# Two small edits to a hybrid GLA and MLP block: more tiny buffers ahead of the second MLP product's operands, and one engine for each PSUM bank of transposed tokens

## The chip, the cores and the metric

The kernel runs on one core of a Trainium2 chip. A core has TensorE (PE in the profile, with its weight loads apart as PEld), VectorE (DVE), ScalarE (ACT), GpSimd (POOL) and SyncE (SP, which here issues nearly all DMAs). The metric is the device time of one execution in microseconds. Three timed runs of the kernel before gave 2401.96, 2402.1 and 2409.05 us; the median is 2402.1 us.

## The reference, cut to what matters

One layer (DEPTH 1) over 2048 latent tokens and 256 context tokens of width 1024: a normed and modulated input goes through bidirectional gated linear attention (GLA), then through a squared-ReLU MLP of width 4096, each added to the residual; a last RMSNorm gives the output.

```python
a_lat = modulate(rmsnorm(h_lat, norm1_g[i]), mod_l[0], mod_l[1])
a_ctx = modulate(rmsnorm(h_ctx, norm1_g[i]), mod_c[0], mod_c[1])
o_ctx, o_lat = gla_mixer(a_ctx, a_lat, gla_w_in[j], ..., gla_w_o[j], need_ctx)
h_lat = h_lat + mod_l[2] * o_lat
h_lat = h_lat + mod_l[5] * sqrelu_mlp(modulate(rmsnorm(h_lat, norm2_g[i]), mod_l[3], mod_l[4]),
                                      mlp_w1[i], mlp_w2[i])
return rmsnorm(h_lat, final_g)

def sqrelu_mlp(h, w1, w2):
    return jnp.square(jax.nn.relu(h @ w1)) @ w2
```

## The kernel before, in words

Every large product is done in fp32r with both operands split into a high and a low part, and three matmuls for each pair (`mm3`, lines 83 to 87: high by high, high by low, low by high). In these calls the first operand named is the stationary one (it is loaded into the array, PEld) and the second is the moving one, which streams through. The profile prints them the other way round: `yp<-w,hs` is a product into `yp` with `w` moving and `hs` stationary.

The program has four stages, one after another.

1. Attention's first stage, from 0 to some 866 us: projections and the backward scan, chunk by chunk, with the partial results stored in DRAM (`sp_d`, `q_d`). Its matmuls have 256 columns.
2. Attention's second stage, from some 866 to 1130 us, over 16 chunks of 128 tokens. `front(ch)` loads `uu`, `o`, `rr` and `qf` of a chunk, advances the forward states `xf0` to `xf3` with `uu` (line 705) and makes `o`. `turn_o` transposes `o` on PE through two PSUM tiles `pt` (line 724) and splits it into `onh` (ACT, line 725) and `onl` (DVE, line 726). `back(ch)` multiplies `onh` and `onl` (stationary) by `wo` (moving, 512 columns), adds the residual, and norms to `hn`. `turn(ch - 1, hn)` transposes `hn` of the chunk before through two PSUM tiles `pt` as well (line 777), and empties them into `a2` with the scale and shift of the second norm: eight instructions of 128x128, four on ACT (line 782) and four on DVE (line 785). `give` then splits the result for the MLP.
3. The MLP's first product, 1130 to 1758 us: seven Strassen products, with slices of `w1` stationary and the tokens (`h2` and `ht`) moving, 512 columns, then the squared ReLU (`sq`).
4. The MLP's second product, 1760 to 2391 us: seven Strassen products again. `load_hs` brings `hs` (stationary) and `load_w2` brings `w` (moving, 512 columns); 2688 matmuls in all. The adds, the last norm and the output follow for each block of tokens.

The order on each engine is set by the tile framework's scheduler, which goes by the order of the code and by the offsets of `tc.high_priority`. A buffer of a pool that is used again waits for its readers. The pool `pw` of the second stage has two PSUM banks, and both `turn` and `turn_o` take their `pt` from it: each uses two, so PE can put the transposes of `o` into a bank only when ACT and DVE have emptied it of `hn`. The framework also keeps two engines from working on one PSUM bank at a time: the first ACT instruction on a bank of `turn` waits for the DVE instruction ahead of it, and the next DVE instruction for ACT. `uu` has one buffer, so the DMA for the next chunk's `uu` starts when the last of the four instructions of line 705 has read it.

A pool's buffers lie one behind another in SBUF, in the order in which the pools are opened. In the last stage `n_w` (the moving `w`) comes first, then `n_x`, then `n_wk` with the small tiles (`junk`, `ssq`, `rsv`, `rsr`, `tmp`), then `n_wr`, `n_hr`, `n_acc` and `n_h` (the stationary `hs`). So the count of `ssq` buffers, each of which takes 32 bytes in a partition, sets the byte at which all that follows begins. `ssq` holds sums of squares (line 1106 and line 1115).

Of the kernel before, what the change touches and what calls it, by code (L numbers as in the profile page):

```python
# [8 lines left out]
F32 = mybir.dt.float32  # L9
# [8 lines left out]
P = 128  # L18
# [19 lines left out]
def kernel(  # L38
# [110 lines left out]
    def held(shape, dtype, name, n):  # L149
        return [hold.tile([P] + shape, dtype, tag="hb", name=name) for _ in range(n)]  # L150
# [10 lines left out]
    with ExitStack() as sa:  # L161
# [3 lines left out]
        wk = sa.enter_context(tc.tile_pool(name="a_wk", bufs=2))  # L165
# [492 lines left out]
    with ExitStack() as sb:  # L658
        wkx = sb.enter_context(tc.tile_pool(name="b_wkx", bufs=2, reuse_waits="tile"))
        wk2 = sb.enter_context(tc.tile_pool(name="b_wk2", bufs=2, reuse_waits="tile"))  # L660
        wk = sb.enter_context(tc.tile_pool(name="b_wk", bufs=2, reuse_waits="tile"))
# [97 lines left out]
        def give(b, cp, i, src):  # L759
            if b == 0 and i in (IB11, IB21, IT1):  # L760
                if cp == 0:
                    h2_block(i)
                for j in range(2):
                    dh, dl = (t_[j][:, cp] for t_ in h2[i])
                    nc.scalar.copy(dh, src[:, 2 * j:2 * j + 2])
                    nc.gpsimd.tensor_sub(dl, src[:, 2 * j:2 * j + 2], dh.bitcast(F32))
            else:
                nc.sync.dma_start(t_d[b, i, cp], src)

        def turn(ch, hn):  # L770
            b, cp = ch // (2 * NCP), ch // 2 % NCP
            a_, = held([2, 4, P], F32, "a2", 1)
            for k4 in range(2):
                pt = pw.tile([P, 4, P], F32, tag="t", name="pt")
                for kk in range(4):
                    k = 4 * k4 + kk
                    nc.tensor.transpose(pt[:, kk, :], hn[:, k * P:(k + 1) * P], ident)
                a2 = a_[:, k4]
                for kk in range(4):
                    k = 4 * k4 + kk  # L780
                    if kk % 2:
                        nc.scalar.activation(a2[:, kk], pt[:, kk], AF.Identity, scale=s2[:, k:k + 1],
                                             bias=b2[:, k:k + 1])
                    else:
                        nc.vector.tensor_scalar(a2[:, kk], pt[:, kk], s2[:, k:k + 1], b2[:, k:k + 1],
                                                op0=ALU.mult, op1=ALU.add)
                if ch % 2 == 0:
                    give(b, cp, (IB11, IB21)[k4], a2)
            if ch % 2 == 0:
                even[0] = a_  # L790
                return
            e_ = even[0]
            t1 = wkx.tile([P, 4, P], F32, tag="t1", name="t1", bufs=1)
            nc.vector.tensor_sub(t1, a_[:, 0], e_[:, 0])
            give(b, cp, IT1, t1)
            nc.vector.tensor_sub(e_[:, 0], a_[:, 1], t1)
            give(b, cp, IT2, e_[:, 0])
            give(b, cp, IB22, a_[:, 1])
            nc.vector.tensor_sub(a_[:, 0], a_[:, 1], a_[:, 0])
            give(b, cp, IT3, a_[:, 0])  # L800
            nc.vector.tensor_sub(e_[:, 1], e_[:, 1], e_[:, 0])
            give(b, cp, IT4, e_[:, 1])
# [10 lines left out]
        for ch in range(1, NCH):  # L813
            if ch == NCH - 1:
                first_w.append(load_w1(0))
            nxt = front(ch + 1) if ch + 1 < NCH else None
            hn, on = back(ch, *on, hn, o_next=nxt)
        turn(NCH - 1, hn)

    scst.close()  # L820
# [189 lines left out]
    with ExitStack() as sm:  # L1010
        wp = sm.enter_context(tc.tile_pool(name="n_w", bufs=16, reuse_waits="tile"))
        xp = sm.enter_context(tc.tile_pool(name="n_x", bufs=2, reuse_waits="tile"))
        wk = sm.enter_context(tc.tile_pool(name="n_wk", bufs=2, reuse_waits="tile"))
# [9 lines left out]
        def load_w2(i, f):  # L1023
            raw = wr.tile([P, 512], F32, tag="wr", name="w2r")
            if i in (1, 2, 3):
                f_, n = ((f, 0), (f + NFP, 0), (f + NFP, 1))[i - 1]
                nc.sync.dma_start(raw, mlp_w2[f_ * P:(f_ + 1) * P, n * 512:(n + 1) * 512])
            else:
                nc.sync.dma_start(raw, wt_d[{5: 0, 6: 1, 7: 2, 4: 3}[i], f])
            w_ = wp.tile([P, 2, 512], F32R, tag="w", name="w2")  # L1030
            nc.scalar.copy(w_[:, 0], raw)  # L1031
            (nc.vector if f % 4 else nc.gpsimd).tensor_sub(w_[:, 1], raw, w_[:, 0].bitcast(F32))  # L1032
            return w_[:, 0], w_[:, 1]

        def load_hs(b, i, q, fq):
            raw = hr.tile([P, FQ, 256], F32, tag="hr", name="hsr")
            n = {1: 0, 2: 1, 4: 2, 5: 3, 6: 4, 7: 5, 3: 6}[i]
            nc.sync.dma_start(raw, hs_d[b, n, q, :, fq * FQ:(fq + 1) * FQ, :])
            h_ = hp.tile([P, 2, FQ, 256], F32R, tag="h", name="hs")
            nc.scalar.copy(h_[:, 0], raw)  # L1040
            nc.vector.tensor_sub(h_[:, 1], raw, h_[:, 0].bitcast(F32))  # L1041
            return h_[:, 0], h_[:, 1]
# [22 lines left out]
        for b in range(NB):  # L1065

            acc = [[None] * 4 for _ in range(2)]
            ssqs = [None] * 4
            for i in (1, 2, 6, 5, 3, 7, 4):
                w2 = []  # L1070
                for q in range(2):
                    yps = [py.tile([P, 512], F32, tag="y", name="yp") for _ in range(2)]
                    for fq in range(NFP // FQ):
                        with tc.high_priority(offset=150):
                            if q == 0:
                                w2 += [load_w2(i, fq * FQ + f) for f in range(FQ)]
                            hi, lo = load_hs(b, i, q, fq)
                        for f in range(FQ):
                            wh, wl = w2[fq * FQ + f]
                            for s in range(2):  # L1080
                                sl = slice(s * P, (s + 1) * P)
                                mm3(yps[s], hi[:, f, sl], lo[:, f, sl], wh, wl, fq == 0 and f == 0,
                                    fq == NFP // FQ - 1 and f == FQ - 1)
                    if b == 0 and i == 1 and q == 0:
                        nc.sync.dma_start(g2t.rearrange("p n e -> p (n e)"), g_d[1])
                        nc.sync.dma_start(fgt.rearrange("p n e -> p (n e)"), final_g.partition_broadcast(P))
                    for s in range(2):
                        t = 2 * q + s
                        ps = yps[s]
                        row0 = b * MB + 2 * t * P  # L1090
                        row1 = row0 + P
                        if i == 1:
                            acc[1][t] = acp.tile([P, 2, 512], F32, tag="acc", name="acc")
                            nc.scalar.copy(acc[1][t][:, 0], ps)
                        elif i == 2:
                            acc[0][t] = acp.tile([P, 2, 512], F32, tag="acc", name="acc")
                            nc.vector.tensor_add(acc[0][t][:, 0], ps, acc[1][t][:, 0])
                        elif i == 6:
                            nc.vector.tensor_add(acc[1][t][:, 0], ps, acc[1][t][:, 0])
                        elif i == 5:  # L1100
                            nc.vector.tensor_add(acc[1][t][:, 1], ps, acc[1][t][:, 0])
                        elif i == 3:
                            a = acc[0][t]
                            nc.vector.tensor_add(a[:, 1], ps, acc[1][t][:, 1])
                            residual(row0, a)
                            ssq = wk.tile([P, 3], F32, tag="ssq", name="ssq", bufs=6)
                            sumsq(a, ssq, 0)
                            sumsq(a, ssq, 1)
                            finish(row0, a, ssq)
                        elif i == 7:  # L1110
                            a = acc[1][t]
                            nc.vector.tensor_add(a[:, 0], ps, a[:, 0])
                            nc.vector.tensor_add(a[:, 1], ps, a[:, 1])
                            residual(row1, a)
                            ssqs[t] = wk.tile([P, 3], F32, tag="ssq", name="ssq", bufs=6)
                            sumsq(a, ssqs[t], 1)
                        else:
                            a = acc[1][t]
                            tmp = wk.tile([P, 512], F32, tag="tmp", name="tmp")
                            nc.vector.tensor_mul(tmp, ps, g2t[:, 0])  # L1120
                            nc.vector.tensor_add(a[:, 0], tmp, a[:, 0])
                            sumsq(a, ssqs[t], 0)
                            finish(row1, a, ssqs[t], b == NB - 1 and t == 3)
# [29 lines left out]
```

## Time and profile before

The profiled execution took 2402.64 us, of which 2400.9 us are the span from its first to its last instruction. The mean granted clock of TensorE in it is 0.987 of full speed.

| engine | busy us | share of the span | instructions |
|---|---|---|---|
| PE | 2305.0 | 96% | 13250 |
| PEld | 2002.9 | 83% | 13250 |
| DVE | 1618.3 | 67% | 2410 |
| ACT | 1233.4 | 51% | 2223 |
| POOL | 525.5 | 22% | 658 |

The DMA engines moved 456.82 MB in the span, 190 GB/s in the mean. Matmuls overlap in this profile: a 512-column matmul is shown with 0.39 us while the next starts some 0.23 us after it, so the pace of PE is read from the starts of matmuls or from how many fall into a stretch, not from their durations.

### The profile page before, as it was taken

To read this page: it belongs to the slowest core of one execution; us is meant where nothing else is said; L and a number is where in the kernel's file an instruction comes from. 1 tells how busy PE (TensorE), PEld (TensorE's weight loads), DVE (VectorE), ACT (ScalarE), POOL (GpSimd) and SP (SyncE) were. 2 spreads that over 40 slices of the span, in tenths; PEclk is the share of its full clock that TensorE was granted. 3 is DMA by queue.
4 is the path that set the end of the run, shared out by engine and by line. 5 is a ranking of instruction groups with operands and counts; after the bars stand their busy time and mean duration, and the time that the engine had idled before them with its cause. 6 is when DMAs were issued, how large, how long until landed. Compare 5 with 4: busy or idle time off the path is not lost.

```text
span 2400.9 us, 36220 instructions
## 1 busy us (share of the span) xinstructions
PE 2305.0 (96%) x13250; PEld 2002.9 (83%) x13250; DVE 1618.3 (67%) x2410; ACT 1233.4 (51%) x2223; POOL 525.5 (22%) x658
## 2 busy tenths in 40 slices
PE   6999999999999988999899999999999999999998
PEld 4899999999999977777688887888878888888886
DVE  7855777787765577777866768766565458554484
ACT  6544455555555545554655556555454344443351
POOL 2333344334433423321000000000011121211131
PEclk8999999999999989999999999999999999999999
DMA  8222454454433266775966678676596458655471
GB/s 275 87 89 95 140 175 155 149 172 141 159 121 117 84 218 209 237 259 195 294 202 206 215 225 264 213 228 202 171 327 216 167 188 298 216 194 203 164 272 71
DMA packets 364635, 456.82 MB, mean 190 GB/s; under 512 B 23164, under 2 KB 268996, under 8 KB 364456
## 3 DMA queue, kind: packets, MB, share of 16 engines
q1 hardware_dynamic: 361784, 446.14, 56.1%
q0 software_dynamic: 2416, 8.07, 1.1%
q8 instruction: 104, 1.70, 0.3%
q14 instruction: 75, 0.61, 0.1%
q10 hardware_dynamic: 256, 0.29, 0.0%
HBM read 318.10 MB, written 136.31 MB: 189 GB/s over the span
## 4 chain that ended last, share of the span: by engine, by line
PE 48%; issue 4%; DVE 4%; DMA 4%; POOL 1%; ACT 1%; SPq 0%; POOLq 0%; DVEq 0%; ACTq 0%
PE yp L86 9%; PE yp L85 9%; PE yp L84 9%; PE pa L84 4%; PE pa L86 4%; PE pa L85 4%; PE pb L84 2%; PE pb L86 2%; PE pb L85 2%; DMA uu<-sp_d 2%; PE pc L84 1%; PE pc L86 1%; PE pc L85 1%; DMA w2r<-in_mlp_w_dram 1%; POOL rsr L95 1%
## 5 line engine op out<-in xcount | busy, mean ns | idle before, releaser
L84 PE MATMUL yp<-w,hs 128*128 128x512 f32 x896 | 353.6, 395 | 2.6 <-ACT hs L1040 2.6
L86 PE MATMUL yp<-w,hs 128*128 128x512 f32 x896 | 353.8, 395 | 1.3 <-DVE hs L1041 1.3
L85 PE MATMUL yp<-w,hs 128*128 128x512 f32 x896 | 353.7, 395 | 0.0
L1032 POOL TENSOR_TENSOR w<-w2r,w 128x512 fp32r<-128x512 f32 x56 | 98.3, 1756 | 1050.3 <-ACT w L1031 1035.7
L345 POOL TENSOR_TENSOR wl<-wraw,wh 128x1024 fp32r<-128x1024 f32 x95 | 236.1, 2505 | 207.5 <-ACT wh L343 205.9
L1041 DVE TENSOR_TENSOR hs<-hsr,hs 128x1024 fp32r<-128x1024 f32 x112 | 139.8, 1251 | 146.4 <-ACT hs L1040 146.3
L1040 ACT CAST hs<-hsr 128x1024 fp32r<-128x1024 f32 x112 | 117.0, 1046 | 200.7 <-PE yp L86 140.4
L84 PEld LDWEIGHTS yp<-w,hs 128*128 128x128 f32 x896 | 168.0, 187 | 44.6 <-ACT hs L1040 3.0
L86 PEld LDWEIGHTS yp<-w,hs 128*128 128x128 f32 x896 | 167.9, 187 | 43.2 <-DVE hs L1041 1.7
L85 PEld LDWEIGHTS yp<-w,hs 128*128 128x128 f32 x896 | 167.9, 187 | 41.6
L1031 ACT CAST w<-w2r 128x512 fp32r<-128x512 f32 x224 | 137.1, 618 | 113.4 <-PE yp L86 100.3
L1032 DVE TENSOR_TENSOR w<-w2r,w 128x512 fp32r<-128x512 f32 x168 | 135.9, 823 | 62.3 <-ACT w L1031 59.3
L84 PE MATMUL vps<-wh,ah 128*128 128x256 f32 x576 | 164.5, 286 | 0.4 <-DVE qr L509 0.4
L85 PE MATMUL vps<-wl,ah 128*128 128x256 f32 x576 | 164.1, 285 | 0.0
L86 PE MATMUL vps<-wh,al 128*128 128x256 f32 x576 | 162.9, 283 | 0.0
L84 PE MATMUL kqps<-ah,wh 128*128 128x256 f32 x544 | 155.8, 286 | 0.0
L85 PE MATMUL kqps<-al,wh 128*128 128x256 f32 x544 | 154.8, 285 | 0.0
L86 PE MATMUL kqps<-ah,wl 128*128 128x256 f32 x544 | 154.1, 283 | 0.3 <-DVE wl L345 0.3
L84 PE MATMUL pa<-ht,w 128*128 128x512 f32 x384 | 149.7, 390 | 3.3 <-DVE z L981 1.7
L85 PE MATMUL pa<-ht,w 128*128 128x512 f32 x384 | 149.4, 389 | 0.0
L86 PE MATMUL pa<-ht,w 128*128 128x512 f32 x384 | 149.4, 389 | 0.0
L84 PE MATMUL rps<-wh,ah 128*128 128x256 f32 x512 | 146.3, 286 | 0.0
(1278 smaller groups left out, 6384.3 us busy)
## 6 DMA issues: line engine op xcount, KB each, us to landing
hsr<-hs_d SPq DMA_DIRECT2D x112, 512.0 KB, 4.5
w2r<-in_mlp_w_dram SPq DMA_DIRECT2D x160, 256.0 KB, 5.2
wraw<-in_gla_w_in_dram SPq DMA_DIRECT2D x64, 512.0 KB, 3.6
w1r<-in_mlp_w_dram SPq DMA_DIRECT2D x64, 512.0 KB, 4.6
hs_d<-z SPq DMA_DIRECT2D x128, 256.0 KB, 3.8
w2r<-wt_d SPq DMA_DIRECT2D x128, 256.0 KB, 3.8
hs_d<-hs SPq DMA_DIRECT2D x96, 256.0 KB, 3.1
sp_d<-sp SPq DMA_DIRECT2D x60, 384.0 KB, 2.4
```

The lines of the kernel that those rows point to most:

```text
L84: nc.tensor.matmul(ps, sh, mh, start=start, stop=False, skip_group_check=skip)
L85: nc.tensor.matmul(ps, sh, ml, start=False, stop=False, skip_group_check=skip)
L86: nc.tensor.matmul(ps, sl, mh, start=False, stop=stop, skip_group_check=skip)
L95: nc.gpsimd.tensor_tensor(r[:, :w], v[:, :w], mhalf[:, :w], op=ALU.pow)
L345: eng.tensor_sub(wl[:, half * 4:half * 4 + 4, :], raw, hs.bitcast(F32))
L1031: nc.scalar.copy(w_[:, 0], raw)
L1032: (nc.vector if f % 4 else nc.gpsimd).tensor_sub(w_[:, 1], raw, w_[:, 0].bitcast(F32))
L1040: nc.scalar.copy(h_[:, 0], raw)
L1041: nc.vector.tensor_sub(h_[:, 1], raw, h_[:, 0].bitcast(F32))
```

## The change

`ssq` gets 12 buffers in place of 6. Six more buffers of 32 bytes move everything behind them in the last stage by 192 bytes. In the built programs the six `hs` buffers begin at byte 170464 + 8192 n of each partition before, and at 170656 + 8192 n after; the moving `w` stays at 16544 + 4096 n. Of these addresses the rest by 512 is what the prediction speaks of: `hs` goes from 480 to 160, `w` is at 160, and the slices that single matmuls take are whole multiples of 512 bytes further on. In the third stage both the stationary `w1` and the moving `h2` and `ht` are at 160. In the second stage the stationary `onh` and `onl` and the moving `wo` are both at 480. In the first stage `vps` has both operands at 160, and `pu_` has its moving `v` at 160 and its stationary `kt` at 224. None of these is moved by the change.

In `turn`, the first PSUM tile (k4 = 0) is now emptied by DVE alone and the second (k4 = 1) by ACT alone; before, each was emptied by both in turns.

```diff
@@ turn
-                    if kk % 2:
+                    if k4:
                         nc.scalar.activation(a2[:, kk], pt[:, kk], AF.Identity, scale=s2[:, k:k + 1],
                                              bias=b2[:, k:k + 1])
                     else:
...
@@ last stage, i == 3
-                            ssq = wk.tile([P, 3], F32, tag="ssq", name="ssq", bufs=6)
+                            ssq = wk.tile([P, 3], F32, tag="ssq", name="ssq", bufs=12)
...
@@ last stage, i == 7
-                            ssqs[t] = wk.tile([P, 3], F32, tag="ssq", name="ssq", bufs=6)
+                            ssqs[t] = wk.tile([P, 3], F32, tag="ssq", name="ssq", bufs=12)
```

The counts of instructions are the same on every engine, and POOL and SP have the same order as before. ACT, for the second stage's even chunks (here the one whose tokens are in `a_12013`; the names in brackets are the engines whose progress the instruction waits for):

```order
-L782 ACTIVATE a_12013<-pt,b_96,s_95 128x128 [waits DVE_49] x2
-L765 CAST h_11345<-a_12013 128x256 [waits Activation_49]
+L782 ACTIVATE a_12013<-pt,b_96,s_95 128x128 [waits PE_49]
+L782 ACTIVATE a_12013<-pt,b_96,s_95 128x128 x3
+L765 CAST h_11345<-a_12013 128x256 [waits DVE_49]
 L765 CAST h_11362<-a_12013 128x256 [waits Activation_49]
-L782 ACTIVATE a_12013<-pt,b_96,s_95 128x128 [waits DVE_49] x2
-L765 CAST h_11346<-a_12013 128x256 [waits Activation_49]
+L765 CAST h_11346<-a_12013 128x256 [waits DVE_49]
 L765 CAST h_11363<-a_12013 128x256 [waits Activation_49]
 L725 CAST onh<-pt 128x512 [waits PE_49] x2
```

The four ACT instructions on `pt` stand together now and wait for PE's transposes alone; two of the casts behind them wait for DVE. DVE, for the same chunk (`xf_102` and `xf_103` are the states `xf0` and `xf1`):

```order
 L713 SCALAR_TENSOR_TENSOR o<-o,rsr,rr 128x256 x4
 L745 TENSOR_TENSOR xt<-yp,xt 128x512
-L785 TENSOR_SCALAR a_12013<-pt,s_95,b_96 128x128 x2
+L785 TENSOR_SCALAR a_12013<-pt,s_95,b_96 128x128 x4
 L705 SCALAR_TENSOR_TENSOR xf_102<-xf_102,ff,uu 128x256
-L785 TENSOR_SCALAR a_12013<-pt,s_95,b_96 128x128 x2
 L705 SCALAR_TENSOR_TENSOR xf_103<-xf_103,ff,uu 128x256
 L726 TENSOR_TENSOR onl<-pt,onh 128x512 x2
```

All four DVE instructions on `pt` now stand ahead of the first instruction that needs `uu`; before, two stood behind it. PE, at the second chunk of the second stage, the one place where its order in that stage differs:

```order
 L85 MATMUL yp<-wo_11059,onh 128x512
 L86 MATMUL yp<-wo_11058,onl 128x512
-L724 MATMUL pt<-ident,o 128x128 x4
+L724 MATMUL pt<-ident,o 128x128 x8
 L84 MATMUL yp<-wo_11060,onh 128x512
-L724 MATMUL pt<-ident,o 128x128 x4
 L85 MATMUL yp<-wo_11061,onh 128x512
 L86 MATMUL yp<-wo_11060,onl 128x512
```

The eight transposes of `o` follow each other there as in the other chunks; before, a matmul stood between the two banks.

## Rows read from the trace of the kernel before

**Rows 1.** Windows: us, busy us of each engine, PEclk, DMA share, GB/s.

```profile
900.00:1120.00 220.00, 204.47 (x1052) 166.56 (x1051) 169.52 (x345) 117.95 (x311) 58.56 (x90) 0.99 0.69 231
913.20:916.20 3.00, 3.00 (x10) 2.52 (x11) 1.38 (x2) 1.25 (x3) 0.73 (x1) 0.50 0.13 25
1160.00:1760.00 600.00, 592.57 (x2610) 489.03 (x2608) 416.86 (x637) 351.24 (x587) 3.93 (x3) 1.00 0.69 222
1500.00:1600.00 100.00, 100.00 (x443) 82.79 (x442) 68.77 (x108) 57.21 (x97) 0.00 (x0) 1.00 0.67 214
1770.00:2390.00 620.00, 620.00 (x2659) 496.87 (x2658) 353.10 (x374) 255.23 (x383) 114.25 (x94) 1.00 0.60 209
```

**Rows 2.** Groups by line, PE: count, busy us, mean ns, idle before.

```profile
L84 PE MATMUL yp<-w,hs 128*128 128x512 f32 x896 | 353.6, 395 | 2.6 <-ACT hs L1040 2.6
```

**Rows 3.** Timeline of PE, fourth stage: start us, duration us, instruction.

```profile
1899.75 0.39 PE L84 MATMUL yp<-w,hs 128*128 128x512 f32 x1
...
1902.32 0.39 PE L86 MATMUL yp<-w,hs 128*128 128x512 f32 x1
```

**Rows 4.** Timeline of PE, third stage.

```profile
1702.20 0.39 PE L84 MATMUL pb<-h,w 128*128 128x512 f32 x1
...
1704.92 0.39 PE L84 MATMUL pa<-ht,w 128*128 128x512 f32 x1
```

**Rows 5.** Timeline of PE, second stage.

```profile
1112.08 0.39 PE L84 MATMUL yp<-wo,onh 128*128 128x512 f32 x1
...
1114.80 0.39 PE L84 MATMUL yp<-wo,onh 128*128 128x512 f32 x1
```

**Rows 6.** Timeline of PE, first stage, `vps`.

```profile
420.00 0.28 PE L86 MATMUL vps<-wh,al 128*128 128x256 f32 x1
...
421.79 0.28 PE L86 MATMUL vps<-wh,al 128*128 128x256 f32 x1
```

**Rows 7.** Timeline of PE, first stage, `pu_`.

```profile
425.98 0.28 PE L86 MATMUL pu__5242<-v__5105,kt 128*128 128x256 f32 x1
...
426.32 0.28 PE L86 MATMUL pu__5242<-v__5105,kt 128*128 128x256 f32 x1
```

**Rows 8.** Waits, 900 to 1120 us: total us, times, longest us.

```profile
ACT a L782 <- DVE a L785: 64.5, 26, 4.1
...
DVE xf L705 <- DMA uu<-sp_d: 7.0, 9, 2.3
...
PE pt L724 <- ACT a L782: 6.7, 8, 2.9
```

**Rows 9.** Timeline of PE, 905 to 917 us.

```profile
909.34 0.66 PE L724 MATMUL pt<-ident,o 128*128 128x128 f32 x4 [0.47 <-ACT a L782]
...
913.14 1.12 PE L724 MATMUL pt<-ident,o 128*128 128x128 f32 x4 [2.91 <-ACT a L782]
```

**Rows 10.** Timeline of DVE, 905 to 917 us.

```profile
908.39 0.72 DVE L785 TENSOR_SCALAR a<-pt,s,b 128x128 f32<-128x128 f32 x2
911.39 0.88 DVE L705 SCALAR_TENSOR_TENSOR xf<-xf,ff,uu 128x256 f32<-128x256 f32 x2 [2.28 <-DMA uu<-sp_d]
...
914.91 0.69 DVE L726 TENSOR_TENSOR onl<-pt,onh 128x512 fp32r<-128x512 f32 x1 [0.63 <-ACT onh L725]
```

**Rows 11.** Timeline of all engines, 942 to 962 us.

```profile
942.48 0.72 DVE L785 TENSOR_SCALAR a<-pt,s,b 128x128 f32<-128x128 f32 x2
...
944.71 0.48 DVE L705 SCALAR_TENSOR_TENSOR xf<-xf,ff,uu 128x256 f32<-128x256 f32 x1 [1.52 <-DMA uu<-sp_d]
...
945.55 0.81 ACT L782 ACTIVATE a<-pt,b,s 128x128 f32<-128x128 f32 x2 [1.23 <-DVE a L785]
...
946.07 1.09 PE L724 MATMUL pt<-ident,o 128*128 128x128 f32 x8 [1.14 <-ACT a L782]
...
959.55 0.48 DVE L705 SCALAR_TENSOR_TENSOR xf<-xf,ff,uu 128x256 f32<-128x256 f32 x1 [0.24 <-DMA uu<-sp_d]
```

**Rows 12.** Chain that ended last, 930 to 1010 us: start us, us, piece.

```profile
937.27 7.35 DMA uu<-sp_d
```

## The prediction

> **What bounds the kernel now.** I read the windows of each stage first, to see where PE has idle time, then the timeline of PE in each stage for its pace, then the waits of the second stage and the chain there. In the fourth stage PE never idles: 620.00 us busy of 620 [rows 1]. So the time of that stage is the count of matmuls times their pace, and no engine or DMA sets it; DVE is busy for 353 and ACT for 255 of those 620 us, and the DMA engines for 0.60 [rows 1]. The third stage is nearly the same, 592.57 of 600. The second stage is another kind: PE is busy for 204.47 of 220 us there [rows 1], and the reader should see that what it waits for at `pt` is an ACT instruction of line 782, 6.7 us in eight waits, while ACT for its part waited 64.5 us for DVE's line 785 [rows 8].
>
> **The pace of PE in the two MLP stages.** A window counts the matmuls that run at either edge too, each 0.39 us long [rows 2 to 4], so the pace is the window plus 0.39 us over the count. Fourth stage: 620.39 / 2659 = 233.3 ns. Third stage, in a window without idle time: 100.39 / 443 = 226.6 ns [rows 1]. The starts say the same: 11 steps from 1899.75 to 1902.32 are 2.57 us, 233.6 ns each [rows 3]; 12 steps from 1702.20 to 1704.92 are 2.72 us, 226.7 ns each [rows 4]. The clock is 1.00 in both stretches, the shape is the same (128x128 stationary, 512 columns of fp32r), and neither waits. What differs is where the operands lie: rests of 480 (stationary) and 160 (moving) by 512 bytes in the fourth stage, 160 and 160 in the third.
>
> The second stage tells which of these counts. There both operands have the rest 480, and 12 steps from 1112.08 to 1114.80 are again 2.72 us, 226.7 ns [rows 5]. So a stationary operand at 480 is not slow by itself, nor a moving one at 160 (the third stage has it), nor a moving operand that lies in one piece (the second stage) against one in four pieces (the third). Only the pairing of the fourth stage, 480 against 160, is seen at 233.3. The change makes this pair 160 and 160, the third stage's.
>
> **The change part by part.**
>
> First, `ssq` with 12 buffers. It adds no instruction, DMA or wait; POOL and SP keep their order. It moves `hs`, `w2r`, `hsr` and the accumulators by 192 bytes. Cost of the move: PE's pace goes from 233.3 to 226.6 ns, 6.7 ns for each of the 2659 matmuls of the window, 17.8 us. The 29 others lie in the first microseconds of the stage, where PE waits for the first operands or runs slowly, and I count nothing for them. Bounds: nothing (0), if what I take for the pairing is something else of the fourth stage; 17.8 us if it is the pairing; on the other side see the second rival. I take 17.8, the end to which all three 512-column rows point. What is late next: `hs` and `w` must come 3% faster. The third stage ran with PE full at a DMA share of 0.69 and 222 GB/s, and the fourth needs 209 x 233.3 / 226.6 = 215 GB/s [rows 1], so nothing is late.
>
> Second, the banks in `turn`. Counts and durations stay: four instructions on each engine. Before, ACT's first stands behind DVE's first on the same bank and DVE stands behind its other work, so both banks become free late. After, ACT's four wait for PE alone and are done early; DVE's four take 0.40 + 3 x 0.32 = 1.36 us at a stretch (two take 0.72, the second adds 0.32) [rows 10, 11].
>
> An even chunk, at 942 us: DVE begins at 942.48 and would be done at 943.84. Before, two of its four stood behind an instruction that waited 1.52 us for `uu` (944.71), so ACT's last began after 945.55 and PE, ready at 946.07 - 1.14 = 944.93, waited 1.14 us [rows 11]. That wait goes whole, and with it what follows it: `onh`, `onl`, the residual, `hn`, and the last reader of `uu`. This matters because `uu` has one buffer and its DMA (7.35 us at this place) lies on the chain [rows 12]: what comes sooner here also starts the next `uu` sooner, so the gain isn't given back at once.
>
> An odd chunk, at 958 us: DVE goes on with the differences of tokens, and its own idle time before `uu` is only 0.24 us [rows 11]. Its sum of work is unchanged, and PE then waits for `onl` in place of `pt`. There I win 0.24 us, not PE's wait.
>
> The first place, 905 to 917 us: PE waited 0.47 and 2.91 us [rows 9], and after the second its clock was 0.50, the lower level of 1.2 GHz, for the ten instructions of 913.2 to 916.2 [rows 1]. Four of them are transposes, 0.66 us at the earlier place [rows 9], six are matmuls of 0.227 us; together 2.0 us where 3.00 passed, so the clock cost 1.0. After the change PE waits for DVE's third and fourth at most, 908.39 + 1.04 = 909.4, and doesn't stop between the banks. But `onl` still stands behind the two instructions that wait for `uu` until 911.39: they end at 912.27, and the two of `onl` (0.69 and some 0.6) at 913.5, where the second ended at 915.60 before [rows 10]. I win 2.1 us, not 4.4.
>
> The sum of the second edit: of the 6.7 us of waits, 3.4 are at the first place (2.1 won) and 3.3 at six others. Of the 3.3 I take two thirds, 2.2, as a choice between the even kind (all) and the odd kind (little). Together 4.3 us. Bounds: at the best all 6.7 and the 1.0 of the clock, 7.7. Below nothing: the first reader of `uu` now stands behind two more of line 785, 0.64 us later, in chunks where `uu` has landed already; DVE waited for `uu` 9 times [rows 8], so in some 6 of the 15 chunks it could cost 0.64 each, 3.8 us slower, if every delay went into the chain. I take 4.3, nearer to the rows of waits than to this end, because DVE's sum of work stays. At the last chunk, where weights for the third stage are prepared between the same instructions, one is moved by one place, at most 0.4 us either way; I take 0.
>
> The sum against the profiled execution's own time: 2402.6 - 17.8 - 4.3 = 2380.5 us. That execution stands 0.5 us above the median of 2402.1, so on the median's scale 2380.0 us. The 1.7 us around the span, and the ten microseconds after the last matmul, stay.
>
> **The rivals.**
>
> The address does nothing for PE. For it: nothing in the profile names an address, and the fourth stage differs from the third in other things too (what DVE, ACT and POOL do beside PE). Against it: in the second stage DVE and ACT do yet other things, and the pace is the third stage's. Then only the second edit is left: 2402.1 - 4.3 = 2397.8 us, no change by the bound below. The Trainium skill speaks for this rival: "SBUF — State Buffer", section "Who interferes with whom", gives PE one read port for the moving operand and an independent one for weight loads, and says that PE never waits on anyone; "TensorE: Matmul & The Clock Gate", section "Back-to-back issue gap", makes the gap a matter of the columns alone. By these the two MLP stages would have one pace, and the edit would be worth nothing; the trace has two paces at one shape and one clock, so I give the rule a small chance.
>
> Equal rests are the slow kind. This one ends on the other side. In the first stage, at 256 columns, `vps` with both operands at 160 takes 15 steps in 1.79 us, 119.3 ns [rows 6], and `pu_` with 160 and 224 takes 3 steps in 0.34 us, 113.3 ns [rows 7]. So there the unequal pair is faster by 6.0 ns. If that held in the fourth stage, 2688 x 6.0 = 16.1 us would be lost: 2402.1 + 16.1 - 4.3 = 2413.9 us. It would decide as soon as it cost over 1.6 ns a matmul (4.3 / 2688). Against it: at 512 columns every row goes the other way, and the runs of `pu_` are six matmuls long.
>
> The `uu` loop takes back what `pt` gives. If each of the 14 loads of `uu` became later by the 0.64 us of two more line-785 instructions, the second stage would be 9.0 us longer in place of 4.3 shorter: 2402.1 - 17.8 + 9.0 = 2393.3 us. For it: the chain goes through these DMAs [rows 12]. Against it: where `uu` is waited for, the four are done before it lands (943.84 against 944.71).
>
> The first edit doing other than it says is not a case of its own: the addresses are those of the built program.
>
> **How the numbers follow.** A measurement of this kernel tells about 0.3%, 7.2 us, from no change. Chances: the forecast 0.86; the address does nothing 0.07; the `uu` loop 0.04, which is still faster by 0.4%; equal rests slow 0.03. So faster 0.90, same 0.07, slower 0.03. The likeliest case alone reaches from 2402.1 - 17.8 - 7.7 = 2376.6 to 2402.1 - 17.8 + 3.8 = 2388.1. The range of 8 in 10 takes that in and a little of each side, for a pace that lies between the two levels or a start of the third stage that moves: 2375 to 2391 us.
>
> **What would show it right or wrong.** In the changed kernel's windows, 600 us inside the fourth stage should count 600.39 / 0.2266 = 2649 matmuls instead of 600.39 / 0.2333 = 2573, and starts should stand 226.7 ns apart. If they stand 233.3 apart, the first step is wrong; at 239, the second rival is right. In the second stage the waits of PE at `pt` should nearly vanish and ACT's wait for DVE's line 785 with them, the clock should not fall at 913 us, and PE should wait for `onl` in places instead; if the stage from 900 us to the last `yp<-wo` is longer than before, the `uu` loop has won. The prediction fails as a whole if the fourth stage keeps its length.

## The result, and the profile after

Five runs of the changed kernel have a median of 2375.05 us (2367.91 to 2376.45), five of the kernel before 2402.46 us (2401.96 to 2409.05). The ratio is 0.9876, with a 95% interval of 0.9862 to 0.9889: 29.8 us faster (26.7 to 33.2). The forecast was 22.1 us. From the median before, 29.8 us lead to 2372.7 us, below the range of 2375 to 2391; the plain median after lies on its lower end. The sign and the first edit came out. The second edit gained more than its upper bound of 7.7 us in the profiled pair, and most of it in a place that the prediction had priced at little.

The profiled execution took 2376.45 us (span 2374.7), 26.2 less than that of before. By the first and last matmuls of each stage, this divides as follows.

| piece | before us | after us | difference | forecast |
|---|---|---|---|---|
| start to the second stage's first L777 | 904.2 | 905.8 | +1.6 | 0 |
| from there to the last `yp<-wo` | 225.8 | 214.1 | -11.7 | -4.3 |
| from there to the first `yp<-w,hs` | 630.1 | 632.6 | +2.5 | 0 |
| first to last `yp<-w,hs` | 630.1 | 612.1 | -18.0 | -17.8 |
| the rest of the span | 10.7 | 10.2 | -0.5 | 0 |

The first and the third row are not effects of the change as far as the runs show: over the kernels below the first piece was 902.0 to 906.7 us and the third 630.8 to 635.5 (646.0 in the one with an added pool), whichever the edit.

The fourth stage does what was forecast. Windows of the changed kernel, with the columns of [rows 1] (us, busy us of PE, PEld, DVE, ACT and POOL, PEclk, DMA share, GB/s):

```profile
900.00:1120.00 220.00, 212.94 (x1108) 175.77 (x1107) 169.56 (x351) 121.75 (x322) 65.82 (x94) 1.00 0.72 238
913.20:916.20 3.00, 2.12 (x10) 1.19 (x8) 3.00 (x6) 1.51 (x3) 0.26 (x1) 1.00 0.58 172
1500.00:1600.00 100.00, 100.00 (x443) 82.81 (x442) 66.46 (x104) 56.78 (x95) 0.00 (x0) 1.00 0.65 207
1760.00:2360.00 600.00, 600.00 (x2649) 496.99 (x2648) 356.29 (x375) 256.15 (x384) 115.65 (x94) 1.00 0.62 217
```

600 us inside the fourth stage count 2649 matmuls, the forecast number, and the third stage's pace is as before (443 in 100 us). In the groups by line the change looks small (390 ns each, 395 in [rows 2]), because a matmul is shown longer than the pace:

```profile
L84 PE MATMUL yp<-w,hs 128*128 128x512 f32 x896 | 349.2, 390 | 3.5 <-ACT hs L1040 3.5
```

but in PE's timeline 12 steps take 1900.74 - 1898.02 = 2.72 us, 226.7 ns each, where [rows 3] had 233.6:

```profile
1898.02 0.39 PE L86 MATMUL yp<-w,hs 128*128 128x512 f32 x1
...
1900.74 0.39 PE L86 MATMUL yp<-w,hs 128*128 128x512 f32 x1
```

The surprise is the second stage. Its waits after, from 898 to 1122 us (total us, times, longest us), against [rows 8]:

```profile
ACT a L782 <- PE pt L777: 18.2, 13, 2.2
...
PE pov L85 <- DVE st L702: 6.0, 8, 1.0
...
DVE xf L705 <- DMA uu<-sp_d: 2.8, 2, 1.8
...
PE yp L86 <- DVE onl L726: 0.7, 2, 0.4
...
PE pt L724 <- DVE a L785: 0.4, 1, 0.4
```

ACT's 64.5 us of waiting for DVE's line 785 are gone, and PE's 6.7 us at `pt` but for 0.4, as forecast, and `uu` is waited for twice instead of nine times. But PE's wait for `onl`, which I expected to grow, shrank. It was this before:

```profile
PE yp L86 <- DVE onl L726: 2.9, 5, 0.6
```

The first place went as the prediction had it. The clock no longer falls at 913 us (1.00 in the second window above, 0.50 in [rows 1]), and the second `onl` ends 913.67 + 1.27 = 914.94, or 9.1 us after the stage's first transposes at 905.80, where 9.3 was forecast (913.5 - 904.2) and 11.4 measured before. Timelines of PE and DVE after (start us, us, instruction, idle before and releaser):

```profile
910.36 1.04 PE L724 MATMUL pt<-ident,o 128*128 128x128 f32 x8
...
914.40 0.50 PE L86 MATMUL yp<-wo,onl 128*128 128x512 f32 x1 [0.28 <-DVE onl L726]
```

```profile
912.38 1.36 DVE L705 SCALAR_TENSOR_TENSOR xf<-xf,ff,uu 128x256 f32<-128x256 f32 x2 [1.83 <-DMA uu<-sp_d]
913.67 1.27 DVE L726 TENSOR_TENSOR onl<-pt,onh 128x512 fp32r<-128x512 f32 x2
```

The odd chunks did not. This is the one whose start [rows 11] show, before, in the timelines of PE, DVE and POOL:

```profile
960.10 0.39 PE L86 MATMUL yp<-wo,onl 128*128 128x512 f32 x1
960.91 1.09 PE L724 MATMUL pt<-ident,o 128*128 128x128 f32 x8 [0.42 <-ACT a L782]
...
965.43 0.50 PE L86 MATMUL yp<-wo,onl 128*128 128x512 f32 x1 [0.63 <-DVE onl L726]
...
967.61 0.39 PE L85 MATMUL pov<-st,qf 128*128 128x256 f32 x1 [0.99 <-DVE st L702]
```

```profile
961.78 0.69 DVE L796 TENSOR_TENSOR a<-a,t 128x512 f32<-128x512 f32 x1
962.38 1.24 DVE L799 TENSOR_TENSOR a<-a 128x512 f32<-128x512 f32 x1
963.54 1.23 DVE L801 TENSOR_TENSOR a<-a 128x512 f32<-128x512 f32 x1
964.70 1.27 DVE L726 TENSOR_TENSOR onl<-pt,onh 128x512 fp32r<-128x512 f32 x2
```

```profile
962.19 2.04 POOL L766 TENSOR_TENSOR h<-t,h 128x256 fp32r<-128x256 f32 x2 [5.82 <-ACT h L765]
```

and the same chunk after:

```profile
956.94 0.40 PE L86 MATMUL yp<-wo,onl 128*128 128x512 f32 x1
957.17 1.04 PE L724 MATMUL pt<-ident,o 128*128 128x128 f32 x8
...
960.84 0.40 PE L86 MATMUL yp<-wo,onl 128*128 128x512 f32 x1
...
962.57 0.39 PE L85 MATMUL pov<-st,qf 128*128 128x256 f32 x1 [0.65 <-DVE st L702]
```

```profile
957.85 0.68 DVE L796 TENSOR_TENSOR a<-a,t 128x512 f32<-128x512 f32 x1
958.45 0.68 DVE L799 TENSOR_TENSOR a<-a 128x512 f32<-128x512 f32 x1
959.06 0.68 DVE L801 TENSOR_TENSOR a<-a 128x512 f32<-128x512 f32 x1
959.66 1.27 DVE L726 TENSOR_TENSOR onl<-pt,onh 128x512 fp32r<-128x512 f32 x2
```

```profile
958.05 2.99 POOL L766 TENSOR_TENSOR h<-t,h 128x256 fp32r<-128x256 f32 x2 [5.10 <-ACT h L765]
```

All three waits of PE shrink or go. DVE's lines 799 and 801 (differences of tokens) take 0.68 us each instead of 1.24 and 1.23, and GpSimd's two subtractions of the tile `t1`, beside them, take 2.99 together instead of 2.04.

The rows in brackets also show less than PE loses. 960.91 - 960.10 is 0.81 us, and without a wait the step takes 0.23 (957.17 - 956.94), so the wait cost 0.58 where the row says 0.42: idle time is counted from the matmul's shown end, 0.39 us after its start, not from the pace. Summed in this way, the steps from a `yp` to the transposes of `o` are 12.0 us before (15 steps) and 3.3 after (14, each 0.23 or 0.24): PE lost some 8.7 us at the start of these transposes before and nothing after.

### The profile page after: what moved, and what is told of

It reads as the page before. It is cut to its first block, busy times and chain, and to the rows that moved or that the text cites. A ratio compares the mean times of both kernels' runs of the same rounds, so it can differ in the third digit from the quotient of the medians.

```text
span 2374.7 us, 36202 instructions
## 1 busy us (share of the span) xinstructions
PE 2286.9 (96%) x13250; PEld 2007.2 (85%) x13250; DVE 1612.1 (68%) x2410; ACT 1232.6 (52%) x2223; POOL 532.4 (22%) x658
## 4 chain that ended last, share of the span: by engine, by line
PE 47%; DMA 2%; DVE 1%; ACT 1%; SPq 0%; issue 0%; POOL 0%; DVEq 0%; POOLq 0%; ACTq 0%
PE yp L86 9%; PE yp L84 9%; PE yp L85 9%; PE pa L84 4%; PE pa L86 4%; PE pa L85 4%; PE pb L84 2%; PE pb L86 2%; PE pb L85 2%; DMA traw<-t_d 1%; PE pc L86 1%; PE pc L84 1%; PE pc L85 1%; DMA w2r<-in_mlp_w_dram 1%; DVE ht L858 0%
## 5 line engine op out<-in xcount | busy, mean ns | idle before, releaser
L84 PE MATMUL yp<-w,hs 128*128 128x512 f32 x896 | 349.2, 390 | 3.5 <-ACT hs L1040 3.5
L86 PE MATMUL yp<-w,hs 128*128 128x512 f32 x896 | 349.4, 390 | 1.1 <-DVE hs L1041 1.1
L85 PE MATMUL yp<-w,hs 128*128 128x512 f32 x896 | 349.0, 390 | 0.0
```

Of the source, the lines that this page charges most:

```text
L84: nc.tensor.matmul(ps, sh, mh, start=start, stop=False, skip_group_check=skip)
L85: nc.tensor.matmul(ps, sh, ml, start=False, stop=False, skip_group_check=skip)
L86: nc.tensor.matmul(ps, sl, mh, start=False, stop=stop, skip_group_check=skip)
```

## The experiments

All are read by the matmuls that fall into 580 us of the fourth stage (1780 to 2360 us; the pace is 580.39 us over that count, by the prediction's rule) and by the second stage's length, from its first L777 to the last `yp<-wo`. "Rest" is the byte of `hs` by 512, set by the number of `ssq` buffers; the moving `w` has 160. The first two experiments were timed four times each, all others once.

**Each edit alone.** The bytes (`ssq` 12, the old `turn`):

> Only the 12 ssq buffers, turn as before. Theory (the byte gives PE's pace in the fourth stage, the banks give the rest): 226.7 ns between starts there, the fourth stage 612.5 us from first to last matmul as in the changed kernel, the second stage 226 us from its first transposes of hn as before, in all 18 us faster than before. Rival (the two edits need each other, or code placement gives part): the fourth stage keeps 233 ns, or the whole is over 22 or under 14 us faster.

The banks (`if k4:` in `turn`, `ssq` 6):

> Only the banks in turn, 6 ssq buffers. Theory: the fourth stage at 233.3 ns as before, the second stage 214 us from its first transposes of hn to its last matmul on wo (226 before), in all 10 to 12 us faster. By the prediction's own sum it would be 4.3 us, at most 7.7.

Against the same seven runs of the kernel before (median 2407.34 us) the bytes alone took 2385.44 us, ratio 0.9911 (0.9893 to 0.9928), and the banks alone 2394.44 us, ratio 0.9942 (0.9924 to 0.996). That is 21.4 us (17.3 to 25.8) and 14.0 us (9.6 to 18.3), the second more than the 10 to 12 expected; the product of the ratios is 0.9854, which by their intervals agrees with the change's own 0.9876. Fourth stage and second stage are 610.8 and 220.4 us with the bytes alone, 629.9 and 215.7 with the banks alone. So the edits work apart from each other, each in its own stage, and the banks are worth more than 4.3 us. The point values are larger than what the two stages show (19.3 us in the fourth; 7.7 in the second, against the mean below). The seven runs of the kernel before lay 4.9 us higher than those of the first comparison, and no profile of them was kept, so where these microseconds lie stays open.

The second stage of the kernel before also varies: six runs with the old `turn` gave 220.4 to 225.8 us (mean 223.4), six with the new one and no other change to that stage 212.6 to 215.7 (mean 214.2). The profile that the prediction was read from was the longest of the six. The mean gain is 9.2 us. By chunk (first L777 to the next) it is 2.0 us at the first place and 6.1 in the four odd chunks of the first half, where GpSimd has its two subtractions of `t1`; the three even chunks between them give 1.4, and all that follows loses 0.3. In those four odd chunks PE's loss at `pt` was only 0.5 to 1.3 us together with the old `turn`.

**Which address counts.** `hs` back at 160 with `w` at 352, so that both move by the same 192 bytes:

```diff
+        fl_ = sm.enter_context(tc.tile_pool(name="n_f", bufs=1, reuse_waits="tile"))
+        nc.gpsimd.memset(fl_.tile([P, 48], F32, name="fill"), 0.0)
```

> The kernel before with a filler of 192 bytes ahead of all buffers of the fourth stage and 6 ssq buffers: hs has the rest 160 by 512 as in the changed kernel, but w is moved along to 352, so their distance is that of before. Theory (the distance between moving and stationary operand counts): 233.3 ns a matmul as before. Rival (the byte of the stationary operand alone counts): 226.7 ns.

```profile
1780.00:2360.00 580.00, 580.00 (x2487) 467.80 (x2486) 339.49 (x361) 253.25 (x379) 113.95 (x90) 1.00 0.65 218
```

2487, the pace of before (233.4 ns), though `hs` has the changed kernel's byte. So the byte of `hs` alone doesn't set the pace; what stayed as before is its distance from `w`. (Its 2413.66 us also hold a wait of PE of 10.9 us at the start of this stage, for ACT's line 1033, where the kernel before has 2.6; it says nothing of the pace.) Then the count of `ssq` was varied, in the kernel before (7, 8 and 10) and in the changed one (14, 16, 11 and 13); in these sessions the kernel before took 2404.36 to 2405.57 us.

```diff
-ssq = wk.tile([P, 3], F32, tag="ssq", name="ssq", bufs=12)
+ssq = wk.tile([P, 3], F32, tag="ssq", name="ssq", bufs=14)
...
```

(The second place where `ssq` is made gets the same count.)

> Turn as before, 7 ssq buffers: hs has the rest 0 by 512 (352 from w's 160; 96 by 128). Theory (the pair is fast where the two rests by 512 are equal, slow elsewhere): 233.3 ns a matmul in the fourth stage. Rival (equal rests by 128 do): 233.3 as well. Second rival (any place but that of before is fast): 226.7. Second stage, as in the three runs with the old turn so far: 220 to 226 us.

> Turn as before, 8 ssq buffers: hs has the rest 32 by 512, 128 from w's 160. Theory (equal rests by 512): 233.3 ns a matmul. Rival (equal rests by 128): 226.7 ns. Second stage 220 to 226 us.

> Turn as before, 10 ssq buffers: hs has the rest 96 by 512, 64 from w's 160 on the other side. Equal rests by 512 and equal rests by 128 both say 233.3 ns a matmul; equal rests by 64 says 226.7, against the kernel before, which has 64 by 128 too. Second stage 220 to 226 us.

> The changed kernel with 14 ssq buffers: hs has the rest 224 by 512, 64 beyond w's 160. So far the pace falls smoothly with the distance: 228.9 ns at 64 short of equal, 226.7 at equal. Theory (least at equal, the same on both sides): 228.9 ns a matmul. Rival (the slope goes on past equal): 224.5 ns, and the fourth stage 6 us shorter than in the changed kernel.

> The changed kernel with 16 ssq buffers: hs has the rest 288 by 512, 128 beyond w's 160. Theory (least at equal, the same on both sides): 232.4 ns a matmul, as at 128 short of equal. Rival (the slope goes on): 221 ns.

> The changed kernel with hs 32 bytes before w's place by 256 bytes (ssq with 11 buffers; hs rest 128, w rest 160, by 512). If the pace goes by the size of the distance, near zero is near 226.7 ns: 226.7 to 228.9 ns, fourth stage 612 to 618 us. If only an exact zero gives the low pace: 232 to 234.3 ns, 627 to 631 us. Below 226.0 ns it would beat the changed kernel.

> The changed kernel with hs 32 bytes behind w's place (ssq with 13 buffers; rest 192). If the pace goes by the size of the distance: the same as at 32 bytes before, 226.7 to 228.9 ns. If it rises at once on this side, as 64 behind shows 233.3: 230 to 233.3 ns, fourth stage 621 to 630 us. Below 226.0 ns it would beat the changed kernel.

| `hs` rest by 512 | `hs` less `w`, by 256 | matmuls in 580 us | pace ns | run us |
|---|---|---|---|---|
| 160 (changed kernel) | 0 | 2561 | 226.6 | 2375.05 |
| 192 | 32 | 2488 | 233.3 | 2396.71 |
| 224 | 64 | 2487 | 233.4 | 2393.53 |
| 480 (kernel before) | 64 | 2487 | 233.4 | 2402.46 |
| 0 | 96 | 2478 | 234.2 | 2407.17 |
| 32 | 128 | 2498 | 232.3 | 2397.93 |
| 288 | 128 | 2498 | 232.3 | 2395.64 |
| 96 | 192 | 2535 | 229.0 | 2395.84 |
| 128 | 224 | 2487 | 233.4 | 2392.36 |

The run times in the last column mix both forms of `turn` (the old one in the rows 480, 0, 32 and 96); only the pace is to be compared. The lines of the first neighbours, one below and one above the place of `w`:

```profile
1780.00:2360.00 580.00, 580.00 (x2487) 465.93 (x2486) 340.86 (x362) 247.07 (x371) 110.69 (x88) 1.00 0.62 208
```

```profile
1780.00:2360.00 580.00, 580.00 (x2488) 466.91 (x2487) 339.84 (x360) 250.27 (x375) 110.78 (x88) 1.00 0.63 211
```

The two pairs with equal distance by 256 (224 and 480; 32 and 288) have equal counts, so a rule by 256 bytes fits every row. By 512, as the prediction had it, no two of these rows share a distance, so the runs do not rule that out. None of the rules in the expectations gave the 229.0 ns at 96, and the mirror of it, 224, was expected at 228.9 and came at 233.4. The pace does not grow with the distance: 32 bytes to either side already cost all of it, 192 only a third. Of the eight distances that these buffers allow seven were measured (160 was not), and zero is the only one at 226.6 ns. Why it goes so was not settled. The count of `ssq` also moves `w2r`, `hsr` and the accumulators against `w`, and no run moved `hs` without them. That it is `hs` and `w` that count rests on the third stage (160 and 160) and the second (480 and 480), which run at 226.6 and 226.7 ns with distance zero [rows 1, 4, 5].

**Which engine takes which bank.** The banks swapped (ACT the first, DVE the second; `ssq` 6):

```diff
-                    if kk % 2:
+                    if not k4:
```

> Banks kept apart as in the changed kernel, but ACT empties the first and DVE the second; 6 ssq buffers. Theory (what counts is that neither engine waits for the other on a bank): second stage 214 to 217 us as with the banks alone, DVE idle for no ACT instruction at a bank and the other way round. Rival (it counts that DVE, which is late, has the bank that is filled first): the second stage is 2 us or more longer than that, PE waits for DVE at the second bank.

2397.44 us in one run, against 2404.53 of the kernel before; second stage 214.6 us, as with the change. So it doesn't matter which engine has which bank. In every version with the banks apart DVE also runs its four instructions on `pt` in a row, ahead of the second half of line 705; no run has that order with the banks shared, so the two can't be told apart.

**Where the surplus of the odd chunks comes from.** DVE's lines 799 and 801 run beside GpSimd's line 766. The first test takes GpSimd's part away, by sending the tile `t1` of block 0 to DRAM as the tiles of other products are, in the kernel before and in the changed one (ACT's two casts of it go with it):

```diff
-            if b == 0 and i in (IB11, IB21, IT1):
+            if b == 0 and i in (IB11, IB21):
```

> The kernel before, but the sums t1 of block 0 go to DRAM like the others and are split in the third stage, so that in the second stage's odd chunks ACT has two casts and GpSimd two subtractions less (the third stage loads and splits them instead, so only the second stage is compared). Theory that DVE's two differences of lines 799 and 801 are slowed by GpSimd's subtraction running at the same time: they take 0.68 us in every odd chunk instead of 1.0 in the mean, the second stage is 2 to 5 us shorter. Rival (the odd chunks gained because ACT's and PE's waits at the banks went, and the slow differences cost nothing): the second stage within 1.5 us of before.

> The changed kernel with the sums t1 of block 0 sent to DRAM as in the third run, so that GpSimd has nothing to subtract beside DVE's lines 799 and 801 in the second stage. Theory that GpSimd's share still costs there: second stage 1 to 3 us shorter than 214 to 216. Rival: within 1 us, and the third stage longer by its added splits.

The second leaves GpSimd's two places in its queue and takes only its read of SBUF away. It leaves out the low part of that tile. It was put into the kernel before, and into the changed kernel with two `uu` buffers:

```diff
-                    nc.gpsimd.tensor_sub(dl, src[:, 2 * j:2 * j + 2], dh.bitcast(F32))
+                    if i == IT1:
+                        nc.gpsimd.memset(dl.bitcast(F32), 0.0)
+                    else:
+                        nc.gpsimd.tensor_sub(dl, src[:, 2 * j:2 * j + 2], dh.bitcast(F32))
```

> The kernel before, old turn, but GpSimd's subtraction of line 766 for the tile of block 0 (two in each odd chunk) is replaced by a memset of zeros, so GpSimd reads no SBUF there; it leaves out the low part of that tile. Same queue places and dependencies. Theory (what made the odd chunks of the first half long before is DVE's lines 799 and 801 sharing SBUF with GpSimd's line 766): these two lines fall from 1.0 us mean to 0.70, the odd intervals of the first half fall from the mean of 16.9 us to 15.3 to 16.0, second stage 217 to 220 us. Rival (the waits at the shared banks made the odd chunks long): odd intervals stay 16.7 to 17.1, second stage 220 to 226 us.

```profile
L802 DVE TENSOR_TENSOR a<-a 128x512 f32<-128x512 f32 x6 | 4.1, 685 | 0.0
```

(its lines stand three lower: 802 is 799). Before, it was this:

```profile
L799 DVE TENSOR_TENSOR a<-a 128x512 f32<-128x512 f32 x6 | 6.3, 1050 | 0.0
```

The odd chunks of the first half fall to 15.3 to 15.9 us, as this theory had it, from a mean of 16.9. But the stage stays at 223.3 us, where it had 217 to 220. Its waits (900 to 1124 us):

```profile
PE pt L724 <- ACT a L785: 8.2, 9, 2.5
...
PE yp L86 <- DVE onl L726: 0.4, 1, 0.4
```

PE waits less for `onl` and longer at `pt`. By the steps from start to start, in us of the second stage (each with its 13 to 15 ordinary steps):

| kernel | stage | to `pt` | from `pov` to `onl`'s reader |
|---|---|---|---|
| before, and five with its `turn` (mean) | 223.4 | 9.4 | 5.8 |
| old `turn`, `t1` to DRAM | 221.2 | 13.2 | 2.6 |
| old `turn`, `t1` set to zero | 223.3 | 13.7 | 2.6 |
| changed, and five with its `turn` (mean) | 214.2 | 3.3 | 3.5 |
| new `turn`, `t1` to DRAM | 214.5 | 3.3 | 2.6 |

So without GpSimd beside DVE the whole stage still differs by 221.2 - 214.5 = 6.7 or 223.3 - 214.5 = 8.8 us between the two forms of `turn`, nearly the 9.2 with it. By chunk, however, the difference lies elsewhere (us, first L777 to the next; the last two kernels are those of the next experiment):

| kernel | first chunk | four odd of the first half | three even between | the rest |
|---|---|---|---|---|
| before, and five with its `turn` (mean) | 17.5 | 67.6 | 44.2 | 94.0 |
| old `turn`, `t1` to DRAM | 17.3 | 63.2 | 45.5 | 95.2 |
| old `turn`, `t1` set to zero | 19.4 | 62.4 | 44.5 | 97.0 |
| changed, and five with its `turn` (mean) | 15.5 | 61.5 | 42.8 | 94.4 |
| new `turn`, `t1` to DRAM | 15.0 | 61.3 | 43.8 | 94.5 |
| new `turn`, two `uu` | 14.4 | 64.3 | 42.7 | 96.4 |
| new `turn`, two `uu`, `t1` set to zero | 14.4 | 60.8 | 45.5 | 97.2 |

In the four odd chunks the old `turn` without GpSimd's reads comes within 0.9 and 1.7 us of the changed kernel: 5.2 or 4.4 of their 6.1 us are had without touching the banks. The other way round, the new `turn` with DVE's lines drawn out in all four (two `uu`) takes 2.8 us more than the changed kernel there, and the memset takes 3.5 off it. So by these single runs DVE's lines account for 2.8 to 5.2 of the 6.1 us, and the banks for the rest. With the old `turn` they were drawn out in all 24 such chunks of six runs, with the new one in 3 of 24. How the new `turn` brings that about was not tested. The theory holds for these chunks and falls for the stage: with `t1` set to zero the first chunk takes 19.4 us (15.2 to 19.0 in the six with the old `turn`) and the rest 97.0 (93.4 to 94.6; with the new `turn` 93.2 to 96.3), though the rest has the same instructions as before. What made it longer there, and whether it would again, a single run doesn't show. With the old `turn`, `t1` to DRAM is 4.6 us shorter than the profile of before, in the range expected, but 2.2 shorter than the mean of the six. With the new `turn`, `t1` to DRAM is within 1 us of the changed kernel, as its rival had it. The runs of `t1` to DRAM took 2400.05 us (old `turn`, median of the kernel before 2407.34) and 2377.91 us (new).

**Does `uu` hold the changed kernel?** Two buffers of `uu` in the changed kernel, and the same with GpSimd's memset:

```diff
-            uu = wk.tile([P, NH, HV], F32, tag="u", name="uu", bufs=1)
+            uu = wk.tile([P, NH, HV], F32, tag="u", name="uu", bufs=2)
```

> The changed kernel with two uu buffers in the second stage, so that the load of the next uu doesn't wait for the last reader of this one. Theory that the loop of uu still sets the second stage's length in part: 2 to 6 us shorter than its 214 to 216. Rival (with the banks kept apart, PE sets the pace and uu is hidden): within 1 us of it.

> The changed kernel with two buffers of uu (second stage 217.9 us in the earlier run) and the same memset in place of GpSimd's subtraction; it leaves out the low part of the tile of block 0. Theory (the second buffer only moved DVE's differences back onto GpSimd's reads): lines 799 and 801 at 0.70 us, odd intervals of the first half from 16.1 back to 15.3 or less, second stage 212 to 214.5 us. Rival (the second buffer costs elsewhere, for instance by the DMAs that it lets start early): second stage stays at 217 to 218.5 us.

2381.68 and 2379.54 us, and the second stage is 217.9 us in both, 3.7 longer than with one buffer. Neither expectation for the second buffer alone came out. The wait for `uu` is gone. Lines 799 and 801 were back at 1.0 us in the mean:

```profile
L799 DVE TENSOR_TENSOR a<-a 128x512 f32<-128x512 f32 x7 | 7.0, 999 | 0.0
```

I took that for the cost. The memset brings them to 0.68 and the four odd chunks from 64.3 to 60.8 us, but the other chunks grow by as much and the stage does not move, so the rival held. With the memset PE waits for its second bank of `o` instead, in the waits of 898 to 1122 us:

```profile
PE pt L724 <- DVE a L788: 4.8, 5, 1.3
```

By chunk (table above) the run without the memset loses 2.8 us in the four odd chunks and 2.0 in the rest, and wins 1.1 at the first; why the other chunks take back what the memset gives stays open. No version tried beats the changed kernel.

## Why the prediction was right or wrong

**The pace: right.** -18.0 us in the fourth stage for -17.8. Which pairs of places are slow was not known and not needed: the change makes the two equal, as they are in the third stage. Whether the rests count by 512, as the prediction had it, or by 256 makes no difference to that. The reading that a stationary operand at 480 is not slow by itself, drawn from the second stage, held: with `hs` at 160 and `w` at 352 the pace is as slow as with 480 and 160. The rival that the address does nothing fell: with the bytes alone the stage took 610.8 us.

**The rival of equal rests being slow: wrong.** At 512 columns zero distance is the fastest of the seven. Its rows at 256 columns were a run of six matmuls: over the whole trace of before, the median step within `pu_<-v,kt` is 118 ns (332 steps) and within `vps` 120, so the difference is 2 ns and not 6. No run moved those operands, so what distance does at 256 columns stays open.

**The first place: right, in part by luck.** The end of `onl` came 2.3 us sooner (11.4 to 9.1) for 2.1 forecast, and the clock stayed up. The chunk itself gained 3.4 us in the pair of profiles (18.97 to 15.62 us from the first L777 to the next chunk's). The 2.0 in the mean of six against six is an average of unlike runs: with the old `turn` two had 15.2 and 15.4 us there, the other four 17.8 to 19.0.

**The other chunks: the step that failed.** "Its sum of work is unchanged, and PE then waits for `onl` in place of `pt`. There I win 0.24 us, not PE's wait." The four odd chunks of the first half won 6.1 us in the mean, 1.5 each, where the whole second edit was forecast at 4.3. Three things were wrong in the step. First, DVE's work was taken as fixed: in these chunks lines 799 and 801 were drawn out from 0.68 to 1.24 us by GpSimd's subtractions, and with the new `turn` they mostly are not. That is worth 2.8 to 5.2 of the 6.1 us by the runs above; the rows of before (1.05 us in the mean, 0.68 in the second half, where GpSimd has no `t1`) could have told it. So `onl` came sooner, not at the same time. Second, the wait at `pt` goes whole in odd chunks as in even ones, since ACT's half of the bank no longer stands behind DVE; in these four chunks it was 1.05 us in the profile of before. Third, the wait itself was under-read: 6.7 us of idle time stood for 8.7 us lost by start to start, and two thirds of a part of it was taken. In the pair of profiles the sum is 8.7 at `pt`, 2.5 at `onl`, 1.1 at other readers of `onl` with the lowered clock, less 0.6 elsewhere: 11.7. The even kind went as forecast: no wait at `pt` is left there, and the three in the first half won 1.4 us. That the new `turn` would change which of DVE and GpSimd gives way was not in the forecast; that it went the good way is luck.

**The `uu` loop taking the gain back: wrong.** The waits for `uu` fell from 7.0 to 2.8 us.

**The bounds.** The upper bound of the second edit, 7.7 us, was built from idle time alone; start to start it would have been some 10 (8.7 and the clock's 1.0), which holds the mean gain of 9.2 but not the 11.7 of the profiled pair. The 18.0 and the mean of 9.2 make 27.2 us, inside the measured 26.7 to 33.2.

## What to carry to other kernels

Where PE is full, compare its pace between stages by the starts of matmuls, and try where the operands lie against each other: 32 bytes off the equal place cost 3% of a stage here. Where two engines empty one bank in turns, each one's queue holds up the other; giving each its own bank won 9.2 of 223 us here, whichever had which, some of it (2.8 to 5.2) because DVE's lines no longer lost to GpSimd. Price a wait of PE by start to start, read more than one execution of a stage that varies, and do not take the duration of a DVE line as fixed when GpSimd runs beside it.

## What the runs showed of the hardware that was not expected

The pace of 512-column matmuls at a granted clock of 1.00 has at least four levels here, 226.6, 229.0, 232.3 and 233 to 234 ns. It changes with the distance of the stationary operand from the moving one, with no order by size, and a rule by 256 bytes fits the nine places. The Trainium skill, "SBUF — State Buffer", section "Who interferes with whom", gives PE independent read ports for the two operands and has it wait on no one; these runs differ from that, since the pace goes by where the operands lie (226.6 against 233.4 ns).

DVE and GpSimd do not share evenly. In the kernel before, line 766 starts 0.19 us ahead of line 799 (962.19 and 962.38) and DVE's two lines take 1.24 and 1.23 us; after, it starts 0.40 us ahead (958.05 and 958.45), DVE's lines take 0.68 and GpSimd's pair 2.99 instead of 2.04 us. The Trainium skill, "SBUF — State Buffer", section "Who interferes with whom", says that a DVE instruction with two SBUF inputs contends with a GpSimd instruction that reads SBUF, and that the order of issue decides who blocks. That one of them loses, and that it changes with their order in time, agrees with these rows. Over all runs, GpSimd led by 0.20 us in the 24 such chunks of the six with the old `turn` and in the four of the new `turn` with two `uu`, and DVE lost in all 28; it led by 0.40 us in the 24 of the six with the new `turn`, and DVE lost in 3. So the start alone does not tell which: in the changed kernel's first odd chunk GpSimd has the same lead of 0.40 us, and DVE lost there.

```profile
927.60 1.24 DVE L799 TENSOR_TENSOR a<-a 128x512 f32<-128x512 f32 x1
```

```profile
927.20 2.24 POOL L766 TENSOR_TENSOR h<-t,h 128x256 fp32r<-128x256 f32 x2 [5.28 <-ACT h L765]
```
